# The output projection's weights in two pools, with the first SwiGLU weights split in the memory of the first

## The chip, the cores and the metric

The kernel runs on one core of a Trainium2 chip. A core has TensorE (PE in the profile; its weight loads are PEld), VectorE (DVE), ScalarE (ACT), GpSimd (POOL) and SyncE (SP), which here only issues DMAs. On-chip memory is SBUF (128 partitions) and PSUM (8 banks of 128 x 512 words of 4 bytes). The metric is the device time of one execution in microseconds (us), the median of several runs.

## The reference

One layer of a hybrid backbone over 1024 latent tokens and 256 context tokens, width 1024, all in float32. Cut to what matters here:

```python
y = hybrid_mixer(h_ctx, h_lat, ...)            # two groups of heads, concatenated: (1280, 1024)
x = x + g1 * (y[:, CTX_LEN:] @ w_out)          # the output projection, with a gated residual
h = modulate(rms_norm(x, norm_ffn_g), sh2, sc2)
gate, up = split(h @ w_ffn_in, 2)              # 1024 -> 2 x 2816
x = x + g2 * ((silu(gate) * up) @ w_ffn_out)   # SwiGLU
return rms_norm(x, final_g)
```

## The kernel before

A scheduler turns the program text into one fixed order of instructions for each engine. It goes through a model of time and takes, on each engine, the ready instruction that stands first in the text; `issue_after` puts instructions behind a given one on its engine. On the chip each engine works its list in order. Memory comes from pools that lie on each other like a stack, from the left or from the right; a tile in reused memory waits for the last use of just those tiles that lay there.

Precision: each float32 operand is split into hi (rounded for the fast matmul) and lo (the rest), and a product is hi x hi + hi x lo + lo x hi, three matmuls. A split is one ACT instruction for hi and one VectorE or POOL instruction for lo. `split` (L313 to L315) does it for weights.

**The output projection** (L1067 to L1217) works on eight tiles of 128 tokens. `wo_half(n)` (L1086) loads w_out's columns of half n (512 of them) in eight blocks k of 128 rows, each multiplied by a gain and split. For half 0 the raw blocks lie in the buffers hf and x1, for half 1 in the two woraw tiles. The split blocks of half 0 lie in the pool WO; those of half 1 lie in `slabs` (L1084), parts of the SwiGLU's inputs X that only tiles 3 and 7 will write, and the last two in WO. For a tile l, `op_y` (L1111) loads y, transposes it on TensorE and splits it, and loads the residual xl; `op_mm(y, n)` (L1128) is the 24 matmuls of half n, then VectorE multiplies by the gate (L1136) and adds xl (L1137) to make x1; `op_norm` (L1141) stores x1 to memory (L1143), squares it on ACT (L1145), takes the root (`rsqrt_mean`, L118), scales x1 (L1147 on VectorE, L1148 on ACT), transposes it (L1155) and modulates it into hf (L1159, L1162).

The SwiGLU's input product is done by Strassen's scheme in Winograd's form: seven products of half-size blocks instead of eight. Tokens 0 to 511 (tiles 0 to 3) and 512 to 1023 (tiles 4 to 7) are its two block columns, so tile l is combined with tile l - 4. `op_norm` makes b11 and b21 from a tile of the first four, and t1, t2, t3, t4 and b22 from a tile of the last four, which takes four differences (L1172) and five splits (ACT L1168; lo on L1169). They run on VectorE for tiles 3 and 7 and on POOL for the others. The order of tiles (L1188) is 0 4 1 5 2 6 3 7, each tile's half 0 first, but half 1 first for tile 7. In the text a tile's norm stands between the two halves of the next one.

**The SwiGLU's first products.** After the loop WO and OY are closed, and FW takes their memory (L1201). `ffn_load(f)` (L1206) loads a gate block g and an up block u of w_ffn_in; the first pair is f = 0 and 11. `ffn_w` (L1232) gives the split weights of a product, from g or u, or from one of the sums s1 to s4 that POOL makes (L1244, L1247). Products 1 and 2 read halves of g and multiply b11 and b21; product 5 reads s1 and t1; 6, 7, 4 and 3 follow (L1333). Each has 12 matmuls (L1274 to L1276) for one f.

**The constant ones** (L177) is loaded at the start and stays in SBUF to the end; `ada_rest` and one sum of gates use it in the first part of the kernel.

Of the kernel before, what the change touches and what calls it, by code (L numbers as in the profile page):

```python
# [17 lines left out]
P = 128  # L18
# [19 lines left out]
def build(nc, tc, ap, dbg=None, stop=None, marks=None):  # L38
# [19 lines left out]
    def close(p):  # L58
        p_close.pop(id(p)).close()
# [101 lines left out]
    try:  # L161
# [15 lines left out]
        ones = const("ones", [P, P])  # L177
# [273 lines left out]
        R2 = pool("r2", bufs=2)  # L451
        ada2 = C.tile([P, 2, KT], F32, tag="ada2", name="ada2")
# [686 lines left out]
        held = {}  # L1139

        def op_norm(l, y, tr=("pc", "pc")):  # L1141
# [3 lines left out]
            S.activation(xl, x1, AF.Square, accum_out=ssx)  # L1145
# [3 lines left out]
            sl = slice((l % 4) * P, (l % 4 + 1) * P)  # L1149
            for half in range(2):  # L1150
                pt = bank(tr[half], "x1T")
                hf = OP.tile([P, 4, P], F32, tag="hf", name="hf", bufs=4)
# [11 lines left out]
                held[l // 4, half] = hf  # L1164
                e = V if l % 4 == 3 else G

                def part(n, src):
                    S.activation(xhi(n, l % 4), src, AF.Copy)  # L1168
                    e.tensor_tensor(xlo(n, l % 4), src, xhi(n, l % 4).bitcast(F32), ALU.subtract)  # L1169

                def diff(n, r, p, q, op=ALU.subtract):
                    e.tensor_tensor(r, p, q, op)  # L1172
                    part(n, r)
# [15 lines left out]
        nxt = op_y(0)  # L1189
        for i, l in enumerate(pairs):  # L1190
            y = nxt
            if l != 7:
                nxt = op_y(pairs[i + 1])
# [4 lines left out]
            before = l, y  # L1198
        close(WO)
        close(OY)  # L1200
        FW = pool("fw", bufs=2)  # L1201
        raws = {}

        last_wfi = [None]

        def ffn_load(f):  # L1206
            raws[f] = []
            for j in range(2):
                raw = FW.tile([P, KT, P], F32, tag="wraw", name="wraw", bufs=4)
# [3 lines left out]
        for f in (0, FT // 2):  # L1213
            ffn_load(f)
        banks(**{"f%d" % i: 1 for i in range(8)})
        op_norm(*before, tr=("f3", "f7"))
# [368 lines left out]
```

## Time and profile before

| | |
|---|---|
| median of 3 runs | 1494.27 us (1492.51 to 1500.16) |
| the profiled execution | 1498.08 us |
| its span | 1496.3 us |
| mean granted TensorE clock | 0.978 |
| output projection, TensorE | from 730.4 to 839.1 us |
| first SwiGLU product begins | 843.15 us |
| part of the seven products' loop | to about 1280 us |

The span goes from the first to the last instruction of the profiled execution. Times in views of the trace are microseconds from the start of the span. A row of the timeline has the start, the length, the engine, the line, the operation, what it writes and reads, and in brackets the idle time before it with what ended it. Engines work side by side, so idle time costs something only where the engine that sets the pace has it. A busy TensorE may still be slow: the granted clock is shown for stretches.

### The profile page before, as it was taken

How to read it: one execution, taken by the hardware profiler on the slowest of the kernel's cores; microseconds unless marked ns; L12 is line 12 of the kernel's file. 1: busy time of each engine (PE TensorE's matmuls, PEld its weight loads, DVE VectorE, ACT ScalarE, POOL GpSimd, SP SyncE). 2: the span in 40 equal slices, each digit the busy share in tenths (PEclk: the TensorE clock that was granted, in tenths of full speed). 3: DMA queues.
4: the chain of work that ended last, by engine and by line, in shares of the span. 5: the costliest groups of instructions: out<-in, count | busy, mean ns of one | idle time of the engine just before them, and what ended most of it. 6: DMA issues, size and time to landing. Idle time of an engine off the chain costs nothing.

```text
span 1496.3 us, 24201 instructions
## 1 busy us (share of the span) xinstructions
PE 1408.3 (94%) x8919; PEld 1205.2 (81%) x8919; DVE 973.7 (65%) x1934; ACT 609.2 (41%) x1270; POOL 633.8 (42%) x589
## 2 busy tenths in 40 slices
PE   8999999987879999999799899999999999999997
PEld 2898888975879899998678678877888888788886
DVE  6566788379867445678667776766555554657477
ACT  5543464375442121245444432323333333454445
POOL 0120011376114333234326578989555553335322
PEclk9999999998989999999899999999999999999999
DMA  9536686478678755985643256765222231785862
GB/s 318 209 106 204 187 260 201 149 249 254 188 219 216 266 188 218 371 345 205 223 135 114 85 200 215 254 225 203 106 106 106 106 141 73 238 285 186 296 210 113
DMA packets 173750, 298.15 MB, mean 199 GB/s; under 512 B 43368, under 2 KB 93752, under 8 KB 168256
## 3 DMA queue, kind: packets, MB, share of 16 engines
q1 hardware_dynamic: 121760, 252.12, 49.5%
q10 hardware_dynamic: 49072, 35.83, 7.7%
q0 software_dynamic: 2800, 8.65, 1.6%
q8 instruction: 70, 1.15, 0.3%
q14 instruction: 48, 0.39, 0.1%
HBM read 206.60 MB, written 89.96 MB: 198 GB/s over the span
## 4 chain that ended last, share of the span: by engine, by line
PE 54%; DMA 16%; DVE 11%; POOL 8%; ACT 5%; issue 5%; SPq 0%; ACTq 0%; POOLq 0%; DVEq 0%
PE ffn L1276 7%; PE ffn L1275 7%; PE ffn L1274 7%; PE tm L342 3%; PE tm L343 3%; PE tm L341 3%; PE b L573 3%; PE b L574 3%; PE b L575 3%; DVE wlo L315 2%; DMA raw<-wd 2%; DMA ar<-ad 2%; PE op L1135 1%; PE op L1134 1%; DMA wd<-tw 1%
## 5 line engine op out<-in xcount | busy, mean ns | idle before, releaser
L342 PE MATMUL tm<-wlo,hhi 128*128 128x256 f32 (+1 forms) x704 | 202.1, 288 | 4.7 <-DVE wlo L315 4.7
L341 PE MATMUL tm<-whi,hhi 128*128 128x256 f32 (+1 forms) x704 | 200.6, 288 | 6.2 <-ACT res L499 2.1
L343 PE MATMUL tm<-whi,hlo 128*128 128x256 f32 (+1 forms) x704 | 199.6, 287 | 1.7 <-issue 1.7
L341 PEld LDWEIGHTS tm<-whi,hhi 128*128 128x128 f32 x704 | 133.8, 191 | 10.2 <-ACT xa L354 2.4
L342 PEld LDWEIGHTS tm<-wlo,hhi 128*128 128x128 f32 x704 | 134.6, 191 | 8.0 <-DVE wlo L315 5.8
L1274 PE MATMUL ffn<-t,whi 128*128 128x512 f32 x352 | 137.5, 392 | 2.4 <-ACT t L1168 1.6
L1275 PE MATMUL ffn<-t,whi 128*128 128x512 f32 x352 | 137.8, 391 | 1.3 <-DVE t L1169 1.3
L1276 PE MATMUL ffn<-t,wlo 128*128 128x512 f32 x352 | 137.6, 392 | 0.8 <-DVE wlo L315 0.8
L343 PEld LDWEIGHTS tm<-whi,hlo 128*128 128x128 f32 x704 | 134.2, 192 | 2.8 <-issue 1.9
L314 ACT ACTIVATE whi<-wraw 128x512 fp32r<-128x512 f32 (+2 forms) x98 | 75.2, 772 | 144.9 <-PE ffn L1275 81.3
L314 ACT ACTIVATE whi<-ws 128x512 fp32r<-128x512 f32 x88 | 55.6, 632 | 166.0 <-PE ffn L1275 128.4
L1401 PE MATMUL fo<-wlo,ahi 128*128 128x512 f32 x308 | 120.0, 390 | 1.3 <-DVE wlo L315 1.3
L315 DVE TENSOR_TENSOR wlo<-wraw,whi 128x512 fp32r<-128x512 f32 (+2 forms) x92 | 104.8, 1141 | 24.0 <-ACT whi L314 24.0
L1400 PE MATMUL fo<-whi,ahi 128*128 128x512 f32 x308 | 119.3, 389 | 0.7 <-ACT ahi L314 0.7
L315 DVE TENSOR_TENSOR wlo<-ws,whi 128x512 fp32r<-128x512 f32 x88 | 93.1, 1059 | 40.0 <-ACT whi L314 39.7
L1402 PE MATMUL fo<-whi,alo 128*128 128x512 f32 x308 | 119.0, 390 | 0.0
L1274 PE MATMUL ffn<-b,whi 128*128 128x512 f32 x264 | 103.7, 393 | 3.9 <-ACT whi L314 3.9
L1276 PE MATMUL ffn<-b,wlo 128*128 128x512 f32 x264 | 103.9, 393 | 2.1 <-DVE wlo L315 2.1
L1275 PE MATMUL ffn<-b,whi 128*128 128x512 f32 x264 | 103.4, 392 | 0.0
L573 PE MATMUL b<-hhi,whi 128*128 128x512 f32 (+1 forms) x256 | 96.3, 376 | 3.6 <-ACT y L577 3.6
L575 PE MATMUL b<-hhi,wlo 128*128 128x512 f32 (+1 forms) x256 | 95.4, 373 | 0.0
L574 PE MATMUL b<-hlo,whi 128*128 128x512 f32 (+1 forms) x256 | 95.3, 372 | 0.0
(428 smaller groups left out, 3493.4 us busy)
## 6 DMA issues: line engine op xcount, KB each, us to landing
adaw<-ada_w SPq DMA_DIRECT2D x48, 512.0 KB, 5.5
pk<-sd SPq DMA_DIRECT2D x16, 1536.0 KB, 10.1
wraw<-wfi SPq DMA_DIRECT2D x44, 512.0 KB, 4.2
ar<-ad SPq DMA_DIRECT2D x33, 512.0 KB, 5.4
w<-wfo SPq DMA_DIRECT2D x22, 512.0 KB, 6.4
wd<-tw SPq DMA_DIRECT2D x11, 1024.0 KB, 4.9
ad<-act SPq DMA_DIRECT2D x20, 512.0 KB, 2.7
raw<-wd SPq DMA_DIRECT2D x20, 512.0 KB, 4.4
```

The lines of the kernel that those rows point to most:

```text
L314: S.activation(hi, raw, AF.Copy)
L315: e.tensor_tensor(lo, raw, hi.bitcast(F32), ALU.subtract)
L341: T.matmul(o, hhi[:, k, tsl], whi[:, k % 4, :], start=(k == 0), stop=False)
L342: T.matmul(o, hhi[:, k, tsl], wlo[:, k % 4, :], start=False, stop=False)
L343: T.matmul(o, hlo[:, k, tsl], whi[:, k % 4, :], start=False, stop=(k == KT - 1))
L573: T.matmul(o, whi[:, k, :], hh, start=(k == 0), stop=False)
L574: T.matmul(o, whi[:, k, :], hl, start=False, stop=False)
L575: T.matmul(o, wlo[:, k, :], hh, start=False, stop=(k == KT - 1))
L1274: T.matmul(o, whi[:, k, :], xhi(xn, slice(0, 4), k), start=(first and k == 0), stop=False, **kw)
L1275: T.matmul(o, whi[:, k, :], xlo(xn, slice(0, 4), k), start=False, stop=False, **kw)
L1276: T.matmul(o, wlo[:, k, :], xhi(xn, slice(0, 4), k), start=False, stop=(k == 3), **kw)
L1401: T.matmul(po[g][i], ahi[:, ts], wlo, start=False, stop=False, **kw)
```

## The change

- **ones** lies in R2, a pool of the kernel's first part, and is loaded where R2 is opened. That frees 512 bytes in each partition for the rest.
- **Weights of the projection.** Half 0 is split into WO (now only these 16 tiles), half 1 into ten slabs of t1, t2, t3, t4 and b22, into the tile woraw0 (the last hi) and into a pool of its own, WO1 (five tiles). The raw blocks of half 0 lie in x1 and xl instead of hf and x1. hf has three buffers instead of four, yt two instead of three.
- **Order.** Tiles 0 1 4 2 5 3 6 7, each with half 0 first. After half 0 of tile 7 WO is closed and FW opened in its memory; `early_loads` loads the g blocks of f = 11 and 0, splits the four weights of products 1 and 2, and loads the two u blocks; then comes half 1 of tile 7. The square of tile 7 is put behind the last of these splits on ACT.
- **Differences.** The last four tiles no longer keep the first four's hf: b11 and b21 are read back as hi and lo, which makes six differences instead of four. Tiles 3, 6 and 7 have theirs on VectorE, but t3 and b22's lo are always on POOL. All of the last four split the modulation between VectorE and ACT.
- **SwiGLU pools.** Split weights are pairs (hi, lo) in one tile, four in FW and every fifth in FX, a second pool that also holds the sums ws, m1, u2 and c22 and is opened after the projection. Products 1 and 2 run f = 11 before f = 0.

```diff
-        ones = const("ones", [P, P])
...
         R2 = pool("r2", bufs=2)
+        ones = R2.tile([P, P], F32, tag="ones", name="ones", bufs=1)
+        S.dma_start(ones, ap["ones"])
...
+        WO1 = pool("wo1", side="right")
         WO = pool("wo", side="right")
...
-        slabs = [X[n][:, i, 3].rearrange("p k t -> p (k t)") for n in X for i in range(2)]
+        slabs = [X[n][:, i, 3].rearrange("p k t -> p (k t)") for n in ("t1", "t2", "t3", "t4", "b22") for i in range(2)]
...
             if n == 0:
-                raws = [OP.tile([P, 4, P], F32, tag="hf", name="hf", bufs=4).rearrange("p k t -> p (k t)")
-                        for _ in range(4)]
-                for _ in range(2):
-                    x1 = OP.tile([P, D], F32, tag="x1", name="x1", bufs=2)
-                    raws += [x1[:, 0:512], x1[:, 512:1024]]
+                raws = []
+                for tag in ("x1", "xl"):
+                    for _ in range(2):
+                        x1 = OP.tile([P, D], F32, tag=tag, name=tag, bufs=2)
+                        raws += [x1[:, 0:512], x1[:, 512:1024]]
...
-                    x.append(slabs.pop(0) if n and slabs else
-                             WO.tile([P, 512], F32R, tag="wo%s%d%d" % (nm, n, k), name="wo" + nm, bufs=1))
+                    if n and slabs:
+                        x.append(slabs.pop(0))
+                    elif n and k == KT - 1 and nm == "hi":
+                        x.append(OR.tile([P, 512], F32R, tag="woraw0", name="wohi"))
+                    else:
+                        x.append((WO1 if n else WO).tile([P, 512], F32R, tag="wo%s%d%d" % (nm, n, k), name="wo" + nm, bufs=1))
...
-                yt = load(OY, dy[l, :, half * 512:half * 512 + 512], "yt", 3, (P, 512))
+                yt = load(OY, dy[l, :, half * 512:half * 512 + 512], "yt", 2, (P, 512))
...
-            S.activation(xl, x1, AF.Square, accum_out=ssx)
+            with tc.issue_after(hold) if hold is not None else nullcontext():
+                S.activation(xl, x1, AF.Square, accum_out=ssx)
...
-                    if l % 4 == 3 and i % 2:
+                    if l > 3 and i % 2:
...
-                e = V if l % 4 == 3 else G
+                A = V if l in (3, 6, 7) else G
...
                 elif half == 0:
-                    held["t1"] = OP.tile([P, 4, P], F32, tag="hs", name="hs", bufs=1)
-                    diff("t1", held["t1"], hf, held[0, 0])
+                    b12 = hf
+                    hi, lo = both("b11")
+                    A.tensor_tensor(t, hf, hi, ALU.subtract)
+                    A.tensor_tensor(t, t, lo, ALU.subtract)
+                    part("t1", t)
                 else:
-                    t1, b21, b12 = held["t1"], held[0, 1], held[1, 0]
-                    diff("t2", t1, hf, t1)
-                    diff("t3", b12, hf, b12)
-                    diff("t4", b21, b21, t1)
-                    part("b22", hf)
+                    A.tensor_tensor(t, hf, t, ALU.subtract)
+                    part("t2", t)
+                    G.tensor_tensor(b12, hf, b12, ALU.subtract)
+                    part("t3", b12, G)
+                    hi, lo = both("b21")
+                    A.tensor_tensor(t, hi, t, ALU.subtract)
+                    A.tensor_tensor(t, t, lo, ALU.add)
+                    part("t4", t)
+                    part("b22", hf, G)
...
+        F1 = (FT // 2, 0)
+        wcount = [0]
+
+        def w_tile():
+            wcount[0] += 1
+            pl, tag, n = (FX, "wx", 1) if wcount[0] % 5 == 0 else (FW, "w", 4)
+            return pl.tile([P, 2, 4, P], F32R, tag=tag, name="w", bufs=n)
...
+        def early_loads():
+
+            for f in F1:
+                raws[f] = [raw_tile()]
+                SY.dma_start(raws[f][0], ap["wfi"][f])
+            hold = None
+            for an, c in (("a11", 0), ("a12", 4)):
+                for f in F1:
+                    w2 = w_tile()
+                    hold = S.activation(w2[:, 0], raws[f][0][:, c:c + 4], AF.Copy).ins
+                    V.tensor_tensor(w2[:, 1], raws[f][0][:, c:c + 4], w2[:, 0].bitcast(F32), ALU.subtract)
+                    early[f, an] = w2[:, 0], w2[:, 1]
+            for f in F1[::-1]:
+                raws[f].append(raw_tile())
+                last_wfi[0] = SY.dma_start(raws[f][1], ap["wfi"][FT + f]).ins
+            return hold
...
-        pairs = (0, 4, 1, 5, 2, 6, 3, 7)
...
-            op_mm(y, int(l == 7))
-            if before:
-                op_norm(*before)
-            op_mm(y, int(l != 7))
+        tiles = (0, 1, 4, 2, 5, 3, 6, 7)
...
+            op_mm(y, 0)
+            if before:
+                op_norm(*before)
+            if l == 7:
+                close(WO)
+                FW = pool("fw", bufs=2)
+                last_split = early_loads()
+            op_mm(y, 1)
             before = l, y
-        close(WO)
+        close(WO1)
         close(OY)
-        FW = pool("fw", bufs=2)
+        FX = pool("fx", bufs=2)
...
-            whi, wlo = ffn_w(f, an)
+            whi, wlo = early.pop((f, an)) if (f, an) in early else ffn_w(f, an)
...
-            for f in ORDER[:2]:
+            for f in F1 if i < 3 else ORDER[:2]:
```

More of the change, by code (lines that the diff above doesn't have):

```diff
@@ L1137, in op_mm, with op_norm @@
             V.tensor_tensor(x1[:, ns], x1[:, ns], xl[:, ns], ALU.add)
-        held = {}
-        def op_norm(l, y, tr=("pc", "pc")):
+        def op_norm(l, y, tr=("pc", "pc"), hold=None):
             _, _, xl, x1 = y
@@ L1148, in op_norm @@
             S.activation(x1[:, 512:1024], x1[:, 512:1024], AF.Copy, scale=rs)
-            sl = slice((l % 4) * P, (l % 4 + 1) * P)
+            if l == 7:
+                last = OP.tile([P, 2, 4, P], F32, tag="xl", name="last", bufs=2)
+                t = last[:, 0]
+            elif l > 3:
+                t = OP.tile([P, 4, P], F32, tag="hs", name="hs", bufs=1)
             for half in range(2):
                 pt = bank(tr[half], "x1T")
-                hf = OP.tile([P, 4, P], F32, tag="hf", name="hf", bufs=4)
+                hf = last[:, 1] if l == 7 and half == 0 else OP.tile([P, 4, P], F32, tag="hf", name="hf", bufs=3)
                 for i in range(4):
@@ L1163, in op_norm, with part, both @@
                                         ALU.mult, ALU.add)
-                held[l // 4, half] = hf
-                e = V if l % 4 == 3 else G
-                def part(n, src):
+                A = V if l in (3, 6, 7) else G
+                def part(n, src, e=A):
                     S.activation(xhi(n, l % 4), src, AF.Copy)
                     e.tensor_tensor(xlo(n, l % 4), src, xhi(n, l % 4).bitcast(F32), ALU.subtract)
-                def diff(n, r, p, q, op=ALU.subtract):
-                    e.tensor_tensor(r, p, q, op)
-                    part(n, r)
+                def both(n):
+                    return xhi(n, l % 4).bitcast(F32), xlo(n, l % 4).bitcast(F32)
                 if l < 4:
@@ L1177, in op_norm, with raw_tile @@
                 elif half == 0:
-                    held["t1"] = OP.tile([P, 4, P], F32, tag="hs", name="hs", bufs=1)
-                    diff("t1", held["t1"], hf, held[0, 0])
-                else:
-                    t1, b21, b12 = held["t1"], held[0, 1], held[1, 0]
-                    diff("t2", t1, hf, t1)
-                    diff("t3", b12, hf, b12)
-                    diff("t4", b21, b21, t1)
-                    part("b22", hf)
-        before = None
-        pairs = (0, 4, 1, 5, 2, 6, 3, 7)
[L1189 to L1193, printed above, removed]
-            op_mm(y, int(l == 7))
-            if before:
-                op_norm(*before)
-            op_mm(y, int(l != 7))
-            before = l, y
-        close(WO)
-        close(OY)
-        FW = pool("fw", bufs=2)
-        raws = {}
-        last_wfi = [None]
+                    b12 = hf
[3 more added lines that the diff above has]
+                    part("t1", t)
+                else:
+                    A.tensor_tensor(t, hf, t, ALU.subtract)
[7 more added lines that the diff above has]
+                    part("b22", hf, G)
+        before = None
+        raws, early = {}, {}
+        last_wfi = [None]
+        F1 = (FT // 2, 0)
[4 more added lines that the diff above has]
+            return pl.tile([P, 2, 4, P], F32R, tag=tag, name="w", bufs=n)
+        def raw_tile():
+            return FW.tile([P, KT, P], F32, tag="wraw", name="wraw", bufs=4)
         def ffn_load(f):
@@ L1208, in ffn_load @@
             for j in range(2):
-                raw = FW.tile([P, KT, P], F32, tag="wraw", name="wraw", bufs=4)
+                raw = raw_tile()
                 last_wfi[0] = SY.dma_start(raw, ap["wfi"][j * FT + f]).ins
                 raws[f].append(raw)
-        for f in (0, FT // 2):
-            ffn_load(f)
+        def early_loads():
[14 more added lines that the diff above has]
+        tiles = (0, 1, 4, 2, 5, 3, 6, 7)
+        nxt = op_y(0)
+        for i, l in enumerate(tiles):
+            y = nxt
+            if l != 7:
+                nxt = op_y(tiles[i + 1])
+            op_mm(y, 0)
+            if before:
+                op_norm(*before)
+            if l == 7:
+                close(WO)
+                FW = pool("fw", bufs=2)
+                last_split = early_loads()
+            op_mm(y, 1)
+            before = l, y
+        close(WO1)
+        close(OY)
+        FX = pool("fx", bufs=2)
         banks(**{"f%d" % i: 1 for i in range(8)})
-        op_norm(*before, tr=("f3", "f7"))
+        op_norm(*before, tr=("f3", "f7"), hold=last_split)
         checkpoint("op")
@@ L1245, in ffn_w @@
                 if (f, n) not in sums:
[L1246 removed]
+                    r = FX.tile([P, 4, P], F32, tag="ws", name="ws", bufs=4)
                     G.tensor_tensor(r, a[p], a[q], op)
@@ L1251, in ffn_w @@
                 src = a[n]
-            hi = FW.tile([P, 4, P], F32R, tag="whi", name="whi", bufs=5)
-            lo = FW.tile([P, 4, P], F32R, tag="wlo", name="wlo", bufs=5)
+            w2 = w_tile()
+            hi, lo = w2[:, 0], w2[:, 1]
             split(src, hi, lo, V)
@@ L1388, in build @@
         for j in range(1, 4):
-            slot = [FW.tile([P, 4, P], F32R, tag=tag, name=nm, bufs=5).rearrange("p (o k) t -> p o (k t)", o=1)
-                    for nm, tag in (("whi", "whi"), ("wlo", "wlo"), ("ahi", "whi"), ("alo", "wlo"))]
+            slot = [x[:, i].rearrange("p (o k) t -> p o (k t)", o=1) for x in (w_tile(), w_tile()) for i in range(2)]
             fo_load(1, [j], slot, raw_of(FE, 1), last_wfi[0])
```

6 lines of the change are left out of this document (3 added, 3 removed).

## The prediction

> **What bounds the kernel now.** I read the page's first lines, then the busy time of each engine in stretches around the change, then TensorE's timeline there, then who keeps it waiting. The page says that TensorE (PE) is the bound:
>
> ```profile
> span 1496.3 us, 24201 instructions
> PE 1408.3 (94%) x8919; PEld 1205.2 (81%) x8919; DVE 973.7 (65%) x1934; ACT 609.2 (41%) x1270; POOL 633.8 (42%) x589
> ```
>
> So only TensorE's idle or slow time can be won, and the change touches one region of it: the output projection (730 to 839 us) and the first SwiGLU products after it. Columns of the next view: stretch, its length, busy time and count of PE, PEld, DVE, ACT, POOL, the granted clock, DMA.
>
> ```profile
> 763.00:839.00 76.00, 75.98 (x380) 63.14 (x380) 54.93 (x121) 32.46 (x60) 42.92 (x31) 1.00 0.38 132
> ...
> 838.90:843.10 4.20, 0.35 (x2) 0.00 (x0) 4.03 (x6) 4.15 (x10) 4.20 (x4) 1.00 0.82 315
> ...
> 846.00:850.50 4.50, 4.48 (x11) 3.52 (x12) 4.43 (x7) 0.00 (x0) 2.85 (x2) 0.50 0.00 0
> 850.50:859.80 9.30, 9.27 (x45) 7.42 (x43) 4.94 (x11) 5.37 (x11) 2.70 (x2) 1.00 0.01 2
> 859.80:863.40 3.60, 0.73 (x2) 0.30 (x2) 3.60 (x5) 2.03 (x4) 2.24 (x2) 1.00 0.00 0
> 863.40:867.60 4.20, 4.17 (x12) 3.33 (x13) 4.13 (x5) 1.42 (x3) 1.04 (x1) 0.60 0.72 239
> ```
>
> The projection itself is full (75.98 of 76.00 us). The loss sits in the junction, 839 to 868 us, in two stalls with a slow stretch behind each. TensorE's timeline names them, and the waits from 870 us to the end, complete in four rows, show that nothing later takes a gain back:
>
> ```profile
> 843.15 0.50 PE L1274 MATMUL ffn<-b,whi 128*128 128x512 f32 x1 [3.90 <-ACT whi L314]
> 846.02 0.80 PE L1276 MATMUL ffn<-b,wlo 128*128 128x512 f32 x1 [2.13 <-DVE wlo L315]
> ...
> 850.99 0.40 PE L1276 MATMUL ffn<-b,wlo 128*128 128x512 f32 x1
> ...
> 855.76 0.39 PE L1276 MATMUL ffn<-b,wlo 128*128 128x512 f32 x1
> ...
> 861.37 0.73 PE L1274 MATMUL ffn<-t,whi 128*128 128x512 f32 x2 [1.59 <-ACT t L1168]
> 863.43 0.47 PE L1275 MATMUL ffn<-t,whi 128*128 128x512 f32 x1 [1.34 <-DVE t L1169]
> ```
> ```profile
> PE fo L1401 <- DVE wlo L315: 1.3, 1, 1.3
> PE ffn L1276 <- DVE wlo L315: 0.8, 2, 0.4
> PE ffn L1274 <- ACT whi L314: 0.7, 1, 0.7
> PE fo L1400 <- ACT ahi L314: 0.7, 1, 0.7
> ```
>
> **Stall I** waits for the first SwiGLU weights to be split (3.90 + 2.13 us idle, then 4.50 us at a clock of 0.50, 2.25 lost). **Stall II** waits for tile 7's part of t1, which product 5 reads (1.59 + 1.34 us idle, then 4.20 us at 0.60, 1.68 lost). Together 8.3 + 4.6 = 12.9 us. That is the ceiling of the junction. A warm matmul takes (855.76 - 850.99)/21 = 0.227 us.
>
> **Part by part: stall I.** Why it waits:
>
> ```profile
> 833.63 3.33 SPq L1210 DMA_DIRECT2D wraw<-wfi  x4
> ...
> 841.44 1.05 ACT L1145 ACTIVATE xl<-x 128x1024 f32<-128x1024 f32 x1
> ...
> 842.48 0.62 ACT L314 ACTIVATE whi<-wraw 128x512 fp32r<-128x512 f32 x1
> ...
> 837.10 0.85 DVE L1162 TENSOR_SCALAR hf<-x1T,ada 128x128 f32<-128x128 f32 x2 [1.74 <-PE x1T L1155]
> ...
> 841.06 3.23 DVE L1169 TENSOR_TENSOR b<-hf,b 128x512 fp32r<-128x512 f32 x2
> 844.28 1.69 DVE L315 TENSOR_TENSOR wlo<-wraw,whi 128x512 fp32r<-128x512 f32 x1
> ...
> DMA to landing us min/median/max: 3.4/3.5/3.7
> ```
>
> The four raw loads go out over 3.33 us, one each time a k of half 0 has been used for the last time: they lie on its first four k. They landed about 837 to 840.5 us, but the split waits in ACT's queue until 842.48 and in VectorE's behind tile 3's remainders (841.06, 3.23 us). The change puts half 0 of tile 7 first and half 1 (24 matmuls, 5.4 us, and 8 transposes, some 0.9; the row at 855.99 below has 1.04 with its overlap) after it. So the loads go out about 6.3 us earlier, near 827.5, the first two (both g blocks) land by 834, and the four splits (ACT 4 x 0.62, VectorE 4 x 0.69 to 1.69) fit ahead of the last projection matmul at about 839.1 (843.15 - 3.90). Tile 3, whose b11 and b21 product 1 reads, now comes two tiles before the end. The four loads pass tile 6's x1 store in SP's queue; a wait there costs at most their own spacing, some 0.8 us each, and delays only tile 6's norm. I take **stall I to 0**, bounds 0 and 3.
>
> **Stall II.** With no stall I, TensorE runs products 1 and 2 (48 matmuls, 10.9 us) from 839.1 and is through at 850.0; with tile 7's eight transposes at 850.9. Then it needs t1 of tile 7. What VectorE has ahead of that, by the groups of lines from 763 to 866 us (busy, mean ns):
>
> ```profile
> L1172 DVE TENSOR_TENSOR hs<-hf 128x512 f32<-128x512 f32 x1 | 0.7, 692 | 0.0
> L1169 DVE TENSOR_TENSOR t<-hs,t 128x512 fp32r<-128x512 f32 x1 | 1.8, 1770 | 0.0
> ...
> L1172 POOL TENSOR_TENSOR hs<-hf,hs 128x512 f32<-128x512 f32 x3 | 3.9, 1286 | 0.0
> ```
> ```profile
> 842.02 3.40 POOL L1247 TENSOR_TENSOR ws<-wraw 128x512 f32<-128x512 f32 x2
> 845.38 3.47 POOL L1247 TENSOR_TENSOR ws<-ws,wraw 128x512 f32<-128x512 f32 x2
> ...
> 847.04 2.96 DVE L315 TENSOR_TENSOR wlo<-wraw,whi 128x512 fp32r<-128x512 f32 x3
> ...
> 850.52 0.47 DVE L1147 TENSOR_SCALAR x<-x,r1y 128x512 f32<-128x512 f32 x1
> 851.71 0.71 ACT L1148 ACTIVATE x<-x,r1y 128x512 f32<-128x512 f32 x1
> 855.99 1.04 PE L1155 MATMUL x1T<-ident,x 128*128 128x128 f32 x8
> ```
>
> The same VectorE operation takes 0.69 us with POOL idle and 1.6 to 1.77 with POOL at work; POOL's takes 1.29 and 1.70. Tile 6's differences, nine on POOL before, become eight on VectorE (t1 two and a split, t2 one and one, t4 two and one) and three on POOL, and they fall behind tile 6's transposed hf, which takes tile 3's old place (837.10). From 837.3 to tile 7's t1, VectorE has twelve operations that read SBUF: these eight, L1137, the scaling L1147, and two for t1 (one before, since t1 is now formed from hi and lo). Beside them stand about 3.0 us of short ones and of reads from PSUM, 1.5 us in which ACT's scaling (0.71) and the transposes pass the data on, and ACT's hi of t1 (0.6). POOL from 839 has two s1, two s2 and tile 6's three, seven at 1.65 or so, 11.6 us; one VectorE operation fits to each. So seven at 1.65 and five at 0.69: 15.0 + 3.0 + 1.5 + 0.6 = 20.1, **t1 at 857.4**. Stall II is then 857.4 - 850.9 = 6.5 us idle, 0.7 more for its lo, and some 1.6 at the low clock: 8.8 in place of the 12.9. **4.1 us gained.** The old wait of the transposes for TensorE's own late products (scaled at 852.4, turned at 855.99) is in that: it goes with stall I.
>
> In the Trainium skill, "SBUF — State Buffer", section "Who interferes with whom", a VectorE instruction with two SBUF inputs and a GpSimd one that reads SBUF exclude each other for the whole instruction. The rows agree (1.7 and 1.7 in turn). Taken strictly, a pair costs 0.69 + 1.29 = 1.98 by the rows' own solo times; the sum would be 2.3 us later than with 1.65. It speaks against loading VectorE here.
>
> **The smaller edits.** At the start of the stage (SP, VectorE, ACT and POOL by their timelines, then the stretch):
>
> ```profile
> 722.76 0.33 SPq L626 DMA_DIRECT2D xl<-x  x1
> ...
> 729.99 0.72 DVE L1103 SCALAR_TENSOR_TENSOR wolo<-x,gain,wohi 128x512 fp32r<-128x512 f32 x1
> 743.64 0.69 DVE L1137 TENSOR_TENSOR x<-x,xl 128x512 f32<-128x512 f32 x1
> ...
> 741.10 0.71 ACT L1102 ACTIVATE b<-woraw,gain 128x512 fp32r<-128x512 f32 x1
> ...
> 739.01 1.29 POOL L1041 TENSOR_TENSOR oc<-oc,pk 128x512 f32<-128x512 f32 x1 [3.66 <-ACT oc L1038]
> ...
> 740.00:763.00 23.00, 22.18 (x99) 16.94 (x98) 10.90 (x17) 7.19 (x11) 0.88 (x2) 1.00 0.34 114
> ```
>
> The raw weights of half 0 now lie in x1 and xl, so the xl loads (last issued at 722.76) wait for the low splits, until 730.7, with the next tile's yt loads behind them on SP. xl is first read at 743.64, so 13 us cover it. One yt buffer less delays tile 1's loads to the same moment; at most 0.5 us. Half 1's first split came at 741.10, right after POOL's last read of pk (739.01 + 1.29), over whose memory b11 lies; with t1 as the first slab it can come earlier, worth at most the stretch's idle 0.82 us. The last hi, now in woraw0, waits for the low split before it, 0.2 us. I take **+0.4 us gained**, bounds -0.7 and 0.8. Tiles 4 and 5 cost POOL eleven operations each (14 to 19 us at 1.29 to 1.75), every second tile, where two tiles take TensorE about 25 us (each 48 x 0.227 and 16 transposes, 1.8): covered. The load of ones leaves ACT's queue at the start and is issued at R2's opening; its first reader is far behind, so 0, bounds 0.3 either way. In the SwiGLU loop five pairs of split weights stay five pairs; hi is given back one matmul (0.23 us) later, and TensorE waits 3.5 us from 870 us on in all, so 0. The hold puts tile 7's square behind the last split on ACT: that split is due by 838, the square began at 841.44 for want of x1, so 0; if the loads came late, the whole chain to t1 would move with them.
>
> **The sum.** 12.9 - 8.8 + 0.4 = 4.5 us. The profiled execution took 1498.08 us (span 1496.3) and would become 1493.6; against the runs' median of 1494.27, from which I forecast, **1489.8**.
>
> **The rivals.**
> - *VectorE keeps ahead.* The order of instructions is the scheduler's; if it puts tile 7's chain before tile 6's later differences, or POOL's sums fall elsewhere, the twelve run at 0.69: 837.3 + 8.3 + 5.1 = 850.7, no stall II, and the whole 12.9 + 0.4 is won: 1481.0. With up to four of them disturbed, t1 comes by 854 and the time by 1486.7. For it: VectorE was idle for several us between 850 and 860 us (4.94 busy of 9.30). Against it: POOL was busy without a break from 839 to 848.8 us, and stays so.
> - *The splits aren't early.* Queued behind tile 6's parts on ACT and VectorE, they come as late as before: stall I's 8.3 us stay, products 1 and 2 end near 859, and the four splits (2.8 to 6.6 us) push t1 to about 862: 3.5 more. Gain 1.1, **1493** (to 1495). For it: before, exactly that queue held them.
> - *VectorE becomes the bound, slower.* Place: between 837 us and product 5. If all twelve and three splits of s1 and s2 ahead of t1 run at 1.77, t1 is there at 837.3 + 26.6 + 5.1 = 869.0, stall II costs 18.1 + 2.3 = 20.4, and 7.1 us are lost: 1501.4. It costs more than before from t1 at 861.5, that is from a mean of 1.27 us for fifteen, or 1.59 for twelve. Against it: POOL has work for seven such pairs, not fifteen.
>
> **How the numbers follow.** Forecast 0.52 (own range 1486.7 to 1493.3, t1 between 853.9 and 860.3); VectorE ahead 0.27; splits not early 0.12; VectorE the bound 0.09. A measurement tells about 0.5%, 7.5 us: faster means under 1486.8, slower over 1501.7. Faster: the first rival and the edge of the forecast, 0.30. Slower: the worse half of the last and what I haven't thought of, 0.07. Same: 0.63. The range from 1482 to 1497 leaves out the best of the first rival and most of the last, some 0.15.
>
> **What would show it.** Right: raw loads issued by 828 to 831 us; TensorE goes from the last projection matmul into product 1 with under 1 us idle; one stall before product 5, of 5 to 8 us, that waits for t1 (its differences or hi), with VectorE full from 838 us and its operations beside POOL at 1.6 or more; one slow stretch of the clock, not two. Wrong: raw loads near 833, a stall at the first product's lo, no stall at product 5, or idle time of TensorE inside the projection.

## The result, and the profile after

The changed kernel takes **1505.87 us** (median of 10 runs, 1496.71 to 1512.86), the kernel before 1495.38 (10 runs, 1490.74 to 1500.16): ratio **1.0062, interval 1.0035 to 1.0089**, some 9 us slower. Forecast were 1489.8 and a range up to 1497. The profiled execution took 1506.29 us. Head of its page:

```profile
span 1504.5 us, 24223 instructions
...
PE 1410.6 (94%) x8919; PEld 1210.6 (80%) x8919; DVE 978.1 (65%) x1933; ACT 611.3 (41%) x1278; POOL 634.3 (42%) x590
```

No engine has noticeably more to do; the 8 us of span are idle and slow time. TensorE's timeline around the junction (idle time before a row, and what ended it, in brackets):

```profile
842.10 0.40 PE L1141 MATMUL op<-wohi,ylo 128*128 128x512 f32 x1
842.34 1.03 PE L1164 MATMUL x1T<-ident,x 128*128 128x128 f32 x8
843.37 0.47 PE L1318 MATMUL ffn<-b,w 128*128 128x512 f32 x1
...
848.46 0.39 PE L1319 MATMUL ffn<-b,w 128*128 128x512 f32 x1
854.90 1.94 PE L1164 MATMUL x1T<-ident,x 128*128 128x128 f32 x8 [6.05 <-DVE x L1152]
856.49 0.78 PE L1320 MATMUL ffn<-b,w 128*128 128x512 f32 x1
858.36 0.80 PE L1318 MATMUL ffn<-b,w 128*128 128x512 f32 x1 [1.09 <-ACT m L1326]
...
867.53 0.74 PE L1318 MATMUL ffn<-t,w 128*128 128x512 f32 x2 [0.64 <-ACT t L1177]
870.26 0.47 PE L1319 MATMUL ffn<-t,w 128*128 128x512 f32 x1 [1.99 <-DVE t L1178]
```

Stall I is gone: TensorE goes from the projection through tile 6's transposes into product 1 without a pause. (That is this profile's figure. In seven profiles of the variants below, TensorE waits 0.6 to 3.0 us at this place for tile 7's gate multiply, L1142.) A new wait of 6.05 us has come: tile 7's transposes stand in TensorE's list after 23 of the 48 matmuls of products 1 and 2, and the other 25 wait behind them. I measure the junction from the last projection matmul to the end of product 5's wait for lo: 838.87 to 863.43 before, **24.6 us**; 842.10 to 870.26 now, **28.2 us**.

That is 3.6 us. 1.0 of them is no loss: tile 6's transposes (842.34, 1.03 us) now stand behind the last projection matmul, while before those of the tile ahead of the last one stood in front of it, at 836.39. The rest is elsewhere. The projection's last matmul comes 3.2 us later (842.10 against 838.87), and the SwiGLU loop has a new wait. TensorE's waits from 885 to 1270 us (in all, times, longest), TensorE at that place, a window around it, and POOL ahead of it:

```profile
PE ffn L1318 <- ACT w L313: 3.8, 2, 3.3
```
```profile
1009.54 0.39 PE L1320 MATMUL ffn<-b,w 128*128 128x512 f32 x1
1013.27 0.80 PE L1318 MATMUL ffn<-t,w 128*128 128x512 f32 x1 [3.34 <-ACT w L313]
```
```profile
1010.00:1020.00 10.00, 6.73 (x17) 4.92 (x18) 3.98 (x5) 2.27 (x4) 7.95 (x7) 0.66 0.80 275
```
```profile
1004.64 1.74 POOL L1371 TENSOR_TENSOR tw<-w 128x512 f32<-128x512 f32 x1
1006.34 1.28 POOL L1373 TENSOR_TENSOR tw<-w,w 128x512 f32<-128x512 f32 x1
1007.58 1.29 POOL L1372 TENSOR_TENSOR tw<-w,tw 128x512 f32<-128x512 f32 x1
1008.83 1.29 POOL L1288 TENSOR_TENSOR ws<-wraw 128x512 f32<-128x512 f32 x1
1010.08 1.26 POOL L1374 TENSOR_TENSOR tw<-w,tw 128x512 f32<-128x512 f32 x1
1011.30 1.26 POOL L1291 TENSOR_TENSOR ws<-ws,wraw 128x512 f32<-128x512 f32 x1
```

ACT's split is named, but it waits for POOL's last row. POOL works without a gap, and the sum `ws` that the next product needs stands behind sums `tw` that are needed only after the loop. By an estimate from these rows, the wait and the clock of 0.66 after it cost 3.3 + 0.34 x 6.73 = 5.6 us. Before lost 1.5 us to all its waits in this loop.

### The profile page after: what moved, and what is told of

Same layout as the page of the kernel before. It is cut to its first block, busy times and chain, and to the rows that moved or that the text cites. A ratio compares the mean times of both kernels' runs of the same rounds, so it can differ in the third digit from the quotient of the medians.

```text
span 1504.5 us, 24223 instructions
## 1 busy us (share of the span) xinstructions
PE 1410.6 (94%) x8919; PEld 1210.6 (80%) x8919; DVE 978.1 (65%) x1933; ACT 611.3 (41%) x1278; POOL 634.3 (42%) x590
## 3 DMA queue, kind: packets, MB, share of 16 engines
q8 instruction: 70, 1.15, 0.3%
## 4 chain that ended last, share of the span: by engine, by line
PE 66%; DVE 10%; DMA 8%; POOL 8%; issue 4%; ACT 4%; SPq 0%; ACTq 0%; DVEq 0%; POOLq 0%
PE ffn L1319 6%; PE ffn L1318 6%; PE ffn L1320 6%; PE fo L1443 4%; PE fo L1444 4%; PE fo L1445 4%; PE tm L341 4%; PE tm L340 4%; PE tm L342 4%; PE b L574 3%; PE b L575 3%; PE b L576 3%; PE op L1139 2%; PE op L1140 2%; PE op L1141 2%
## 5 line engine op out<-in xcount | busy, mean ns | idle before, releaser
L1318 PE MATMUL ffn<-t,w 128*128 128x512 f32 x352 | 136.3, 394 | 4.5 <-ACT w L313 3.8
L1319 PE MATMUL ffn<-t,w 128*128 128x512 f32 x352 | 138.3, 393 | 2.0 <-DVE t L1178 2.0
L1320 PE MATMUL ffn<-t,w 128*128 128x512 f32 x352 | 137.3, 392 | 0.0
L314 DVE TENSOR_TENSOR w<-ws,w 128x512 fp32r<-128x512 f32 x88 | 92.1, 1048 | 50.4 <-ACT w L313 48.5
L1443 PE MATMUL fo<-whi,ahi 128*128 128x512 f32 x296 | 115.3, 389 | 0.3 <-ACT ahi L313 0.3
L1444 PE MATMUL fo<-wlo,ahi 128*128 128x512 f32 x296 | 115.2, 389 | 0.0
L1445 PE MATMUL fo<-whi,alo 128*128 128x512 f32 x296 | 114.1, 389 | 0.0
L1318 PE MATMUL ffn<-b,w 128*128 128x512 f32 x264 | 103.8, 393 | 1.7 <-ACT m L1326 1.7
L1320 PE MATMUL ffn<-b,w 128*128 128x512 f32 x264 | 103.9, 394 | 0.0
L1319 PE MATMUL ffn<-b,w 128*128 128x512 f32 x264 | 103.4, 392 | 0.0
L313 ACT ACTIVATE w<-ws 128x512 fp32r<-128x512 f32 x88 | 55.0, 627 | 103.1 <-PE ffn L1320 81.6
L584 DVE SCALAR_TENSOR_TENSOR y<-u,cw,y 128x1022 f32<-128x1022 f32 (+3 forms) x80 | 81.3, 1032 | 10.0 <-ACT y L578 9.7
L314 DVE TENSOR_TENSOR wlo<-raw,whi 128x512 fp32r<-128x512 f32 x74 | 63.3, 882 | 37.4 <-ACT whi L313 37.4
```

What stands on the lines that cost most here:

```text
L314: e.tensor_tensor(lo, raw, hi.bitcast(F32), ALU.subtract)
L1318: T.matmul(o, whi[:, k, :], xhi(xn, slice(0, 4), k), start=(first and k == 0), stop=False, **kw)
L1319: T.matmul(o, whi[:, k, :], xlo(xn, slice(0, 4), k), start=False, stop=False, **kw)
L1320: T.matmul(o, wlo[:, k, :], xhi(xn, slice(0, 4), k), start=False, stop=(k == 3), **kw)
L1443: T.matmul(po[g][i], ahi[:, ts], whi, start=(j == 0 and not kw), stop=False, **kw)
L1444: T.matmul(po[g][i], ahi[:, ts], wlo, start=False, stop=False, **kw)
```

## The experiments

"Ratio" is to the kernel before, on the same chip; the runs come from several chips, so variants are compared by their ratios. The junction is as defined above, from one profile each.

| run | time, us | ratio (interval) | junction, us |
|---|---|---|---|
| the changed kernel | 1505.9 | 1.0062 (1.0035 to 1.0089) | 28.2 |
| store6_act | 1507.1 | 1.0072 (1.0049 to 1.0095) | 29.7 |
| lateturn | 1504.8 | 1.0061 (1.0042 to 1.0079) | 29.0 |
| defer6 | 1500.4 | 1.0042 (1.0021 to 1.0064) | 22.7 |
| three | 1505.9 | 1.0085 (1.0048 to 1.0123) | 28.0 |
| wpaced | 1499.1 | 1.0014 (0.9994 to 1.0035) | 30.0 |
| before_wpaced | 1491.7 | 0.9982 (0.9962 to 1.0002) | 23.7 |
| before_ones | 1499.8 | 1.0019 (0.9998 to 1.0040) | 21.6 |
| ones_r1 | 1499.1 | 1.0029 (1.0012 to 1.0047) | 29.2 |
| defer6_wpaced | 1494.6 | 0.9986 (0.9965 to 1.0007) | 23.4 |
| ones_w | 1492.0 | 0.9983 (0.9962 to 1.0005) | 29.5 |
| ones_d6w | 1489.1 | 0.9947 (0.9929 to 0.9965) | 23.9 |
| ones_w_pool6 | 1491.6 | 0.9979 (0.9959 to 1.0000) | 25.7 |
| best2 | 1495.4 | 0.9999 (0.9980 to 1.0018) | 19.6 |
| best5 | 1486.5 | 0.9938 (0.9916 to 0.9960) | 18.7 |

The junction scatters from profile to profile. It is 21.6 to 24.6 us in the three profiles of before's junction (before, before_wpaced, before_ones; mean 23.3) and 28.2 to 30.0 us in the four of the changed one (the changed kernel, wpaced, ones_r1, ones_w; mean 29.2). So the change made it longer by nearer 6 us than 3.6, the 1.0 us of transposes included.

### The junction: whose list holds it up?

Three theories for the late product 5: the raw loads wait behind tile 6's store on SP; tile 7's transposes stand too early on TensorE; VectorE has too much ahead of tile 7's t1.

**store6_act**

```diff
-            SY.dma_start(dx1[l], x1)
+            (S if l == 6 else SY).dma_start(dx1[l], x1)
```

> The changed kernel, with tile 6's x1 store issued from ACT's queue and not from SP's, so that the four raw loads don't stand behind it. Measure: from the last projection matmul's start to the end of product 5's wait for lo: 24.6 us before, 28.2 after. Theory loads (the loads held behind the store on SP make the whole chain late): raw loads issued near 832 us instead of 835.5, the four splits done by 842, tile 7's second add about 2 to 3 us earlier, and the measure falls to 25 to 26; the time by 2 to 3 us. Theory VectorE's list and theory place of the transposes: the loads go earlier, but the measure stays within 1 us of 28.2.

The loads did go out 3.6 us earlier (831.85, not 835.48), and the junction didn't get shorter. ACT's timeline shows why:

```profile
834.77 0.36 ACTq L1147 DMA_DIRECT2D dx<-x  x1
...
842.43 0.72 ACT L1153 ACTIVATE x<-x,r1y 128x512 f32<-128x512 f32 x1 [5.77 <-DMA dx<-x]
843.06 2.17 ACT L1232 ACTIVATE w<-wraw 128x512 fp32r<-128x512 f32 x4
```

The scaling overwrites x1 and so waits for x1's store. Issued behind four loads, the store lands 7.7 us later (842.43 - 834.77); in the changed kernel, ahead of them, 3.0 us (835.07 to 838.05). The Trainium skill says in "DMA: Bandwidth & Descriptors", section "Issuing engines are not separate DMA queues", that DMAs of all issuing engines end up on the same 16 DMA engines; this row agrees. And the splits, whose data are there, stand behind the scaling in ACT's list. What the edit gained on SP it lost on ACT: the splits start at 843.06, in the changed kernel at 839.91. So the run leaves open what earlier loads would be worth if the scaling didn't wait for the store.

**lateturn**: `op_norm(7)` is traced in two parts, the second after product 2 of f = 11, and tile 7's scaling on ACT stands behind m1's copy. The diff is cut to the transposes.

```diff
+                with tc.issue_after(late["turn"]) if "turn" in late else nullcontext():
+                    for i in range(4):
+                        k = half * 4 + i
+                        T.transpose(pt[:, i * P:(i + 1) * P], x1[:, k * P:(k + 1) * P], ident)
...
+                if i == 2 and f == F1[0]:
+                    late["turn"] = end
```

> The changed kernel, with tile 7's eight transposes put behind three of the four products 1 and 2 on TensorE (36 matmuls, not 23) and m1's copy ahead of tile 7's scaling on ACT. VectorE's list ahead of tile 7's t1 keeps its instructions. Theory place of the transposes (they hold TensorE's list for 6.05 us with 25 matmuls ready behind them): the 6 us of idle go, product 5 starts 5 to 6 us earlier, the measure falls from 28.2 to 22 to 23, the time by 5 to 6 us. Theory VectorE's list: t1 comes when it came, the idle time only moves from the transposes to product 5; measure 27 to 28.5, time within 1 us.

As the rival said: nothing gained. But the wait moved to a place that neither theory had named. TensorE, then ACT:

```profile
863.27 0.79 PE L1325 MATMUL ffn<-b,w 128*128 128x512 f32 x1 [9.56 <-ACT m L1334]
...
873.29 0.73 PE L1325 MATMUL ffn<-t,w 128*128 128x512 f32 x2 [1.37 <-ACT t L1164]
```
```profile
862.11 0.63 ACT L1164 ACTIVATE t<-hs 128x512 fp32r<-128x512 f32 x1 [3.27 <-DVE hs L1196]
862.64 0.58 ACT L1334 ACTIVATE m<-ffn 128x512 f32<-128x512 f32 x1
```

Product 2 needs m1's copy, which stands on ACT behind the hi of tile 6's t2, which waits for VectorE. The transposes were moved on TensorE, and VectorE's list came back through ACT.

**defer6**: tile 6's t2 and t4, five VectorE operations with ACT's two hi, behind tile 7's t1. `late7["t1"]` is the lo of tile 7's t1. The diff is cut.

```diff
+                with tc.issue_after(late["diffs"]) if "diffs" in late else nullcontext():
                     A.tensor_tensor(t, hf, t, ALU.subtract)
...
+        late6["diffs"] = late7["t1"]
```

> The changed kernel, with the five VectorE operations of tile 6's t2 and t4 behind tile 7's t1 in VectorE's list; the transposes stay where they are on TensorE. Theory VectorE's list (too many operations ahead of tile 7's t1): its modulation follows the transposes at once, t1 comes 5 to 6 us earlier, the measure falls from 28.2 to 22 to 23 although the 6 us idle ahead of the transposes stay; time 5 to 6 us less. Theory place of the transposes: TensorE's 25 remaining matmuls after them end at 866.9 in any case, so at most 1.5 us are won; measure 26.7 or more.

```profile
852.72 1.94 PE L1176 MATMUL x1T<-ident,x 128*128 128x128 f32 x8 [6.00 <-DVE x L1152]
...
862.67 0.47 PE L1333 MATMUL ffn<-t,w 128*128 128x512 f32 x1 [0.83 <-DVE t L1165]
```

The 6 us ahead of the transposes stay, and the junction still falls by 5.5 us, into the range of before's. So VectorE's list carries the loss; the place of the transposes costs nothing of its own as long as t1 is late. The time falls by 0.20%, 3 us, less than the expected 5 to 6, and the intervals overlap; two further pairs below show the gain more clearly.

**three** joins the edits.

> The three edits together (store from ACT, tile 7's transposes behind three products, tile 6's t2 and t4 behind tile 7's t1). If the three stand one behind the other on one chain, the measure falls to about 16 to 18 us (48 matmuls at 0.23 and the transposes are 12 of it) and the time by 10 us, to the time of before or a little under; if one of them alone carries the loss, it comes out as that one does alone, 22 to 23.

Neither came: 28.0. In its trace m1's copy stands on ACT behind three of tile 6's hi (TensorE idle for 5.50 us), and the scaling of tile 6 again waits for the late store (6.67 us idle on ACT).

### The loop: POOL's order

**wpaced** holds the loads for `w_sums` behind the newest raw load, so that its 44 POOL operations spread over the loop:

```diff
+            with tc.issue_after(last_wfi[0]):
                 SY.dma_start(w0, ap["wfo"][j * P:(j + 1) * P, :])
                 SY.dma_start(w1, ap["wfo"][(j + FH) * P:(j + FH + 1) * P, :])
```

> The changed kernel; the loads for the sums of the second weights (w0, w1) are held behind the raw load traced last, so that POOL makes these sums through the whole loop and not as early as it can. In the changed kernel POOL is full from 974 to 1013 us and a sum ws that product 5 needs stands behind them: TensorE idle 3.3 us, and slow after it. Theory POOL's order in the loop (this is 3 to 5 us of the loss): no idle of TensorE over 1 us between 885 and 1290 us; first to last SwiGLU matmul some 4 us shorter than 446.8; time 3 to 5 us less than the changed kernel's. Theory scatter: that stall is there or not by chance, the time as the changed kernel's within 1.5 us.

**before_wpaced**, the same in the kernel before:

> A control: the kernel before with the paced loads alone. Before loses 1.65 us of TensorE's time to waits in the SwiGLU loop. If the loop's stall of the changed kernel is a loss that the change brought, pacing can win no more than those 1.7 us here: 1493.5 to 1496. If pacing is worth as much here as in the changed kernel (6 us), the loop's loss was there before, and the change isn't to blame for it: 1489 to 1491.

The first 130 us of the loop, changed kernel, then wpaced (fifth pair: POOL):

```profile
880.00:1010.00 130.00, 129.44 (x569) 106.17 (x567) 87.44 (x88) 38.68 (x66) 119.19 (x78) 1.00 0.64 228
```
```profile
880.00:1010.00 130.00, 130.00 (x575) 107.63 (x574) 84.31 (x92) 39.58 (x67) 98.58 (x68) 1.00 0.49 176
```

POOL falls from 119 to 99 of 130 us, TensorE has no wait left, and the time falls by 0.48%, 7 us. The stall itself comes and goes without pacing: TensorE's waits from 885 to 1270 us are 3.4 to 3.9 us in the profiles of the changed kernel, store6_act, defer6 and three, but 2.0 in ones_r1 and 0.4 in lateturn. So what pacing is worth rests on the times. In the kernel before, it wins 0.18% or 2.7 us (interval -0.3 to 5.7). With the three pairs below, which give 0.46 to 0.56%, some 0.3% or 4 to 5 us of the loop's loss belong to the change, and the rest was there. I don't know which of its edits set POOL's order; the sums, the pools and the order of the first products may all bear on it.

### The scans: an edit without a cost of its own

**before_ones** is the kernel before with `ones` in R2; **ones_r1** the changed kernel with `ones` loaded where before loads it, in a pool that has room:

```diff
         R1 = pool("r1", bufs=2)
+        ones = R1.tile([P, P], F32, tag="ones", name="ones", bufs=1)
+        S.dma_start(ones, ap["ones"])
```

> The kernel before with one edit: ones lies in R2 and is loaded there. From the start to the output projection every engine's list is then that of the changed kernel. The profiles of the changed kernel and of its four variants reach the projection's last matmul 1 to 14 us later than the one profile of before. Theory reordering (moving ones reorders the scans' lists and makes them slower): the time is 2 to 5 us over before, and the last projection matmul comes at 841 us or later against 838.9. Theory scatter (that stage varies from run to run, and the order costs nothing): the time within 1.5 us of before; the place in one profile may lie anywhere from 838 to 850.

> The changed kernel with ones in R1 and loaded where before loads it. The lists of all engines ahead of the projection are then those of before; the rest is as in the changed kernel. Theory reordering (moving ones costs some 3 us in the scans): 2 to 5 us under the changed kernel's 1505.9, that is 1501 to 1504. Theory scatter: within 1.5 us of 1505.9.

Moving that one DMA changes the order of the scheduler's lists on PE, VectorE, ACT and POOL up to the projection; with ones_r1 they are in before's order again. before_ones is 0.19% slower, 2.9 us, with an interval that just includes 1; ones_r1 takes 0.33%, 4.9 us, off the changed kernel, though their two intervals overlap. The traces agree in the mean, with much scatter: in the nine profiles with the new order the projection's last matmul comes at 838.0 to 853.0 us, median 841.8, in the seven with the old one at 829.5 to 839.6, median 836.8. (In five of these seven the projection also starts earlier, as follows.) Which wait in the scans makes the difference I could not tell from the scatter, and no run separates the DMA itself from the order that comes with it.

With the old order the change also shows a gain that the reordering hides. The projection's first matmul, before and in ones_w:

```profile
734.14 0.50 PE L1133 MATMUL op<-wohi,yhi 128*128 128x512 f32 x1 [2.71 <-ACT yhi L1122]
```
```profile
727.79 0.50 PE L1139 MATMUL op<-wohi,yhi 128*128 128x512 f32 x1 [0.35 <-ACT yhi L1128]
```

From the last matmul of `ru` (L979, in the variants L980), near the end of the stage ahead, that is 19.0 us in both profiles of the kernel before with the old order, and 15.1 to 16.4 in the five of the changed one with it. In the eight of the changed one with the new order it is 16.9 to 19.1.

### Do the three add up, and is it count or order?

> Both: tile 6's t2 and t4 behind tile 7's t1 on VectorE, and the paced loads. If the junction and the loop are two separate losses, they add: junction 22 to 23 us as in defer6, no stall in the loop, and a time 8 to 10 us under the changed kernel, that is at the time of before or 2 us under it. If the loop only takes back what the junction wins (POOL sets its pace), one of the two gains alone is seen, 5 us.

> The changed kernel with ones in R1 and the paced loads, its junction untouched: the partner of ones_d6w, which differs from it by tile 6's t2 and t4 behind tile 7's t1 alone. Theory junction's own loss (5.5 us in the trace of defer6 arrive in the time): 1493.5 to 1496, that is 4.5 to 6.5 over ones_d6w's 1489.1; junction 28 to 30 us. If the junction's gain was lost again later in defer6 and isn't worth more than 3 us: 1490 to 1492.

> Three repairs of the changed kernel together: ones in R1, tile 6's t2 and t4 behind tile 7's t1, paced loads. If the losses add (scans 3, junction 5.5, loop 5), they come to 13 of the 1505.9 us: 1491 to 1493, 2 to 5 us under before. If the scans' share is scatter: as the two other repairs without it, 1494.6.

Each repair can be read from three pairs of runs that differ in it alone:

| repair | pairs (without, with) | the ratio falls by, % |
|---|---|---|
| ones at its old place | changed, ones_r1; wpaced, ones_w; defer6_wpaced, ones_d6w | 0.33, 0.31, 0.39 |
| paced loads | changed, wpaced; ones_r1, ones_w; defer6, defer6_wpaced | 0.48, 0.46, 0.56 |
| tile 6's t2 and t4 behind tile 7's t1 | changed, defer6; wpaced, defer6_wpaced; ones_w, ones_d6w | 0.20, 0.28, 0.36 |

A single pair is good to about 0.3% either way, worked out from the two intervals, but the three of each repair agree. The means, 0.34, 0.50 and 0.28%, make 1.12%; all three together take 1.15% off (1.0062 to 0.9947). So they add. The junction is 5.6 us shorter in the trace of ones_d6w than in that of ones_w, and 0.36% are 5.4 us of time.

**ones_w_pool6** takes tile 6's eight operations off VectorE and gives them to POOL, as before had them (`A = V if l in (3, 7) else G`).

> As ones_w, with tile 6's differences on POOL, as the kernel before has them: eight VectorE operations fewer ahead of tile 7's t1, and eight more for POOL. Theory count (VectorE has too many operations ahead of t1, and taking them away helps whatever the order): junction 21 to 23 us, time as ones_d6w's 1489 to 1490. Theory contention (POOL beside it makes VectorE's remaining operations as slow as it shortens the list, and tile 6's t1 on POOL comes last): product 5's wait moves to tile 6's t1, junction 25 to 29 us, time 1491 to 1496.

```profile
849.64 1.94 PE L1164 MATMUL x1T<-ident,x 128*128 128x128 f32 x8 [5.61 <-DVE x L1152]
...
859.75 0.73 PE L1318 MATMUL ffn<-t,w 128*128 128x512 f32 x2 [1.28 <-ACT t L1177]
```
```profile
856.53 1.78 DVE L1188 TENSOR_TENSOR last<-last,b 128x512 f32<-128x512 f32 x1
...
859.05 1.69 DVE L316 TENSOR_TENSOR w<-ws,w 128x512 fp32r<-128x512 f32 x1
860.66 1.75 DVE L1178 TENSOR_TENSOR t<-last,t 128x512 fp32r<-128x512 f32 x1
```

The theory of contention was nearer: 25.7 us, and no gain in time that can be told from ones_w. Its other sign didn't come: product 5 still waits for tile 7's t1 (the row at 860.66), not for tile 6's. Eight operations fewer don't help much where POOL then runs beside those that stay (1.7 to 1.8 us each). Doing the urgent ones first, as in ones_d6w, helped more.

### A version better than both

**best2** adds to defer6 and wpaced: the scaled x1 is written to xl, so it waits for no store; the store follows the loads; transposes and m1's copies placed as above; the second pair of early splits behind tile 7's last add; the splits of the sums ws for the first two f behind tile 7's t1, with s1's lo on POOL.

> A version meant to be better than both: the changed kernel with the scaled x1 written to xl (so that it doesn't wait for x1's store), tile 6's store behind the raw loads on SP, the second pair of early splits behind tile 7's last add on VectorE, tile 6's t2 to b22 behind tile 7's t1, tile 7's transposes behind three products, m1's copies ahead of tile 6's remaining splits on ACT, the lo of s1 for the first two f on POOL, and the paced loads. Theory lists (all the junction's loss is the order on four engines): raw loads at 833 or before, no idle over 2 us at tile 7's transposes, from the last projection matmul to product 5's lo 14 to 18 us against 24.6 before, time 6 to 10 us under before (1485 to 1489). Theory VectorE's sum (it has too much to do in any order): that distance stays at 20 or more, and the time within 3 us of before.

best2's junction is 19.6 us, between the two theories' figures, and its time is that of before (0.9999): the 6 to 10 us didn't come.

**best5** has `ones` in R1 too, all four early splits ahead of tile 7's second half, tile 6's modulation behind tile 7's last add, and s2's lo on POOL.

> A version meant to be better than both: as best2, and ones in R1, all four early splits on VectorE ahead of tile 7's second half, tile 6's modulation behind tile 7's last add, and the lo of s1 and s2 for the first two f on POOL. In best2 VectorE was busy for 33.7 of 36 us from 841 to 877, with the second pair of splits (3.48 us) at 843.7 although their data were there at 839. Theory VectorE's sum: these 3.5 us come out of the junction; from the last projection matmul to product 5's lo 15 to 17 us (19.6 in best2, 24.6 before), time 4 to 8 us under before, 1488 to 1492. If something behind the junction takes it back, as in best2: within 2 us of before.

Its SP, VectorE and TensorE:

```profile
820.73 2.39 SPq L1240 DMA_DIRECT2D wraw<-wfi  x2
```
```profile
827.34 2.49 DVE L1247 TENSOR_TENSOR w<-wraw,w 128x512 fp32r<-128x512 f32 x4
831.10 0.69 DVE L1142 TENSOR_TENSOR x<-op,g1r 128x512 f32<-128x512 f32 x1 [1.27 <-PE op L1141]
831.83 1.69 DVE L1143 TENSOR_TENSOR x<-x,xl 128x512 f32<-128x512 f32 x1
```
```profile
840.97 1.09 PE L1183 MATMUL x1T<-ident,xl 128*128 128x128 f32 x8 [0.81 <-DVE xl L1153]
848.24 0.73 PE L1344 MATMUL ffn<-t,w 128*128 128x512 f32 x2 [3.40 <-ACT t L1165]
...
859.42 0.50 PE L1345 MATMUL ffn<-t,w 128*128 128x512 f32 x1 [2.73 <-DVE t L1166]
```

Here the four splits are through at 829.8, in 2.49 us, before the projection's last matmul (830.67), as the prediction had meant it. best5 is 0.62% under before, 9 us, and ones_d6w with three small edits 0.53%: their intervals overlap. The 5 us by which its junction is shorter come back for the most part: product 6 now waits 2.73 us for t2, and from product 5's lo to the end of the loop's matmuls it takes 418.4 us against 413.9.

## Why the prediction was wrong, point by point

**What bounds the kernel.** TensorE, and the two stalls: right. That "nothing later takes a gain back" was wrong. I read it from the waits of before, 3.5 us in all, and didn't read how full POOL is there (119 of 130 us in the changed kernel).

**Stall I to 0.** Right for TensorE, wrong in the way. I had the loads at 827.5 and priced the store on SP that they pass at "some 0.8 us each". The scheduler put the store first:

```profile
835.07 0.32 SPq L1147 DMA_DIRECT2D dx<-x  x1
835.48 1.22 SPq L1227 DMA_DIRECT2D wraw<-wfi  x2
836.75 0.93 SPq L1237 DMA_DIRECT2D wraw<-wfi  x2
```

Loads "near 833" stood among the prediction's own signs of being wrong. The four splits did not end ahead of the last matmul, but at 846.0, on VectorE in the middle of the chain to t1. TensorE didn't see it, because product 1 needs only the first of them at 843.37, and that one ended at 841.3.

**Stall II at 8.8 us.** Here the step failed that I had worked out most closely: "VectorE has twelve operations that read SBUF", 20.1 us from 837.3. t1's hi was there at 867.5, 30.3 us after 837.2. VectorE from 837.3 to 866.6 us by groups of lines (busy, mean ns, idle before):

```profile
L1178 DVE TENSOR_TENSOR t<-hs,t 128x512 fp32r<-128x512 f32 x3 | 4.3, 1419 | 0.8 <-ACT t L1177 0.7
L1233 DVE TENSOR_TENSOR w<-wraw,w 128x512 fp32r<-128x512 f32 x4 | 4.0, 1009 | 2.0 <-ACT w L1232 2.0
L314 DVE TENSOR_TENSOR w<-ws,w 128x512 fp32r<-128x512 f32 x3 | 3.2, 1052 | 0.7 <-ACT w L313 0.7
...
L1188 DVE TENSOR_TENSOR hs<-hf,b 128x512 f32<-128x512 f32 x1 | 1.1, 1107 | 0.1
...
L1189 DVE TENSOR_TENSOR hs<-hs,b 128x512 f32<-128x512 f32 x1 | 0.7, 691 | 0.0
```

| term, us | predicted | measured |
|---|---|---|
| the twelve operations | 15.0 | 12.4 |
| seven splits (L1233 x4, L314 x3) | 0 | 7.2 |
| first half's add, tile 6's scaling | 0 | 1.2 |
| waits of VectorE | 1.5 | 3.8 |
| short ones, reads of PSUM (the rest) | 3.0 | 5.1 |
| ACT's hi of t1 | 0.6 | 0.6 |
| in all | 20.1 | 30.3 |

The price was not too low but too high; the **count** was short by the seven splits. I had put the four early ones ahead of it and left the three of ws out, though the rival beside it had them. And where they stand matters too: tile 7's second add came at 846.28, 3.1 us after its data, and the scaling at 853.29, behind two of tile 6's differences. No run takes these seven away alone; best5 moves all seven, with other edits, and has a junction of 18.7 us. TensorE lost 10.4 us to five waits from 848.9 to 870.3, and more at the low clock:

```profile
854.90:860.00 5.10, 4.01 (x13) 3.21 (x14) 4.30 (x6) 1.63 (x3) 0.98 (x1) 0.50 0.01 3
860.00:867.00 7.00, 6.24 (x22) 4.34 (x20) 6.01 (x10) 4.33 (x10) 2.12 (x2) 0.83 0.00 0
```

That is 0.50 x 4.01 + 0.17 x 6.24 = 3.1 us, so 13.5 in all, where 8.8 were forecast and before had 12.9.

**The port.** Beside POOL the operations took up to 1.8 us; the rows of before had shown 1.6 to 1.77. The Trainium skill says in "SBUF — State Buffer", section "Who interferes with whom", that a VectorE instruction with two SBUF inputs contends with a GpSimd one that reads SBUF; these rows agree. ones_w_pool6 shows what that means here: moving work from VectorE to POOL took little of it out of the way.

**Small edits.** `ones`: "0, bounds 0.3 either way" was the second failed step. With the order that the scheduler makes of it, the kernel took 3 to 5 us longer. The start of the projection was worth 3 us and not 0.4, but only where the scans keep their order. Tiles 4 and 5 on POOL stayed covered (TensorE waits 1.7 us from 738 to 841 us, none of it for POOL). Tile 7's square waited for the second add, not for its hold.

**The loop at 0**: the third failed step, some 4 to 5 us, which holding back POOL's later sums wins back.

**The rivals.** "VectorE becomes the bound, slower" was the right mechanism, and I gave it 0.09, as "POOL has work for seven such pairs, not fifteen". Its t1 at 869.0 is near (hi at 867.5, lo at 870.1), but by luck: it had fifteen operations at 1.77 us, and it was nineteen at 1.03. Nor did POOL stay busy from 839 us on: its first sum ws began at 842.51. "The splits aren't early" was right in that the four splits pushed t1 back, and wrong in that stall I would stay. The longer junction alone brought no measurable loss: ones_w, where only it is left, has 0.9983, and before_wpaced, with the same pacing, 0.9982.

**What adds up to the loss.** In ratios, the order that comes with ones cost 0.34%, the loop 0.32% (0.50 less the 0.18 that pacing wins in before) and the junction 0.28%, as far as its repair shows: 0.94% together, where 0.62% were measured. So something else won some 0.3%, 5 us. The earlier start of the projection is 3 of them; where the rest comes from stays open, and 0.3% is what a single pair is uncertain by.

## What to carry to other kernels

Count every instruction of an engine between two events, also those that the same change puts there for another purpose, and ask for each which must come before the one that the critical engine waits for. Where a scheduler orders the lists, an edit that seems to cost nothing can reorder a stage far from it: compare the lists of both programs on all engines, and load a constant at its old place. After a gain, look at the engine that is full behind it: work that nobody waits for yet (here the sums tw) is best held back until it is due.

## What the runs showed of the hardware that I had not expected

Even an instruction on 128 x 1 elements can be held up beside POOL: the last step of the root, with two inputs, took 0.16 us with POOL idle and 0.92 beside it (up to 1.28 in this trace). The step just ahead of it (L134, a TENSOR_SCALAR) took 0.27 us at both places, and POOL worked at the second one too (851.54 to 853.24).

```profile
837.10 0.16 DVE L138 SCALAR_TENSOR_TENSOR r1y<-r1u,r1y 128x1 f32<-128x1 f32 x1
...
852.34 0.92 DVE L138 SCALAR_TENSOR_TENSOR r1y<-r1u,r1y 128x1 f32<-128x1 f32 x1
```

The scaling L1152, which reads one large operand, went from 0.49 (838.06) to 1.46 us (853.29). A store of 512 KB took 3.0 us to land ahead of four loads of 512 KB and 7.7 us behind them.
